# Expert weights split a whole raw tile at a time: one 2048-element split in place of two of 1024, with four pairs of buffers and six raw tiles

## The chip, the cores and the metric

The kernel runs on one core of one Trainium2 chip. The metric is device time in microseconds (us), the median of several runs. The core's engines are TensorE (PE, with its weight loads as PEld), VectorE (DVE), ScalarE (ACT), GpSimd (POOL) and SyncE (SP), which here issues the DMAs of the weights.

## What is computed

Two layers of a trunk over 272 tokens of width 1024: three token mixers in each layer, then a dense SwiGLU in the first layer and a mixture of eight experts, two per token, in the second. The change touches the experts alone:

```python
def swiglu(h, w_gate, w_up, w_down):
    return (jax.nn.silu(h @ w_gate) * (h @ w_up)) @ w_down

def moe_swiglu(h, router_w, w_gate, w_up, w_down):
    ...                       # top-2 of 8 experts, softmax weights in combine
    out = jnp.zeros_like(h)
    for e in range(N_EXPERTS):
        out = out + combine[..., e:e + 1] * swiglu(h, w_gate[e], w_up[e], w_down[e])
    return out
```

All weights are float32: 1024 x 3584 for gate and up, 3584 x 1024 for down, eight times; 352 MB in all.

## The kernel before

**Split products.** A float32 product is made from products of a shorter type (fp32r). Each operand is split into a high part (rounded) and a low part (the rest). For a piece of raw weights r, ACT writes the high part h (L855), DVE the low part l = r - h (L856), and PE multiplies with both. Every piece thus passes DMA, ACT, DVE and PE in this order.

**Experts.** The eight experts are ordered by their number of tokens. The four largest are "wide" (up to 128 tokens in one side; three products for each block of weights: h, l, and h once more with the tokens' low part, L1106 to L1108), the other four "narrow" (up to 64 tokens, whose high and low part lie side by side; two products: h, l, L1134 and L1135). The inner width 3584 is worked in 7 chunks of 512, so there are 28 wide and 28 narrow chunks. `order` (L1228 to L1231) begins with four wide chunks, then sets one narrow and one wide in turn (24 such pairs), and ends with the narrow ones that are left over.

**One chunk** (L1192 to L1219): two raw tiles of gate weights (g) are multiplied into `psg`, two of up weights (u) into `psu`, each of 1 MB and four blocks of 128 rows; then come two raw tiles of the down weights (d) of the chunk before it, two blocks each. Between them ACT reads the sums: in a narrow chunk `gs` from `psg` (L1140), `us` from `psu` (L1141) and, after PE has turned both (`hps`, L1149), the SiLU `s` (L78); in a wide chunk the SiLU `h` from `psg` (L78), which DVE multiplies by `psu` (L1113), and after PE's transposes `hth` (L1124). These readings stand in the same queues of ACT and DVE as the splits.

**Order.** The programmer writes the work in the order above. A planner of the framework lays out, when the program is built, the order of the instructions on each engine; it goes by its own idea of how long things take, and where the next product in the program's order isn't ready by its clock, it sets a later one that is. On the chip each engine then keeps to that order and waits at the head of its queue. Products into one PSUM tile keep the program's order.

**Buffers.** `RB` raw tiles of 8 KB per partition; `HB` pairs of h and l, of which the last `LATE` lie in a pool of their own. A raw tile is split in pieces of `st` blocks, 1024 elements per partition, so two pieces for each tile. A raw tile is free when both engines have read it, and a pair when PE has used it. The first `EARLY` pieces may be split before the router is done; those after them, up to the 15th, wait in the order for the router's instructions (L858 to L862).

Of the kernel before, what the change touches and what calls it, by code (L numbers as in the profile page):

```python
# [51 lines left out]
def trunk(ctx: ExitStack, tc: tile.TileContext, x, meta, n1g, n2g, w_in, qng, kng, dlam,  # L52
# [12 lines left out]
    def raw_ins(i):  # L65
        return getattr(i, "ins", i)
# [754 lines left out]
                    n1.add(dk, hs[:, dk, :])  # L821


    HB, RB, LATE, YB = 7, 7, 2, 1
    MT = dict(reuse_waits="tile")
    mo = ctx.enter_context(tc.tile_pool(name="mo", bufs=1, **MT))
    wqs = [ctx.enter_context(tc.tile_pool(name=f"wq{i}", bufs=1, **MT)) for i in range(2)]
# [6 lines left out]
        return pw.tile([P, 512], F32, tag="pw", name=name)  # L834

    nparts = [0]
    EARLY = 5

    class MoveWeights:

# [4 lines left out]
            nc.sync.dma_start(self.raw, src)  # L845

        def parts(self):
            st = 1024 // self.cols
            for k0 in range(0, self.nk, st):
                late = nparts[0] % HB >= HB - LATE  # L850
                wq, nb_ = (wqs[0], LATE) if late else (wqs[1], HB - LATE)
                hi = wq.tile([P, st, self.cols], F32R, tag="hi", bufs=nb_, name="h_" + self.name)
                lo = wq.tile([P, st, self.cols], F32R, tag="lo", bufs=nb_, name="l_" + self.name)
                r = self.raw[:, k0:k0 + st, :]
                ih = raw_ins(A.activation(hi, r, AF.Copy))  # L855
                il = raw_ins(V.tensor_tensor(lo, r, hi.bitcast(F32), op=ALU.subtract))  # L856
                nparts[0] += 1
                if EARLY < nparts[0] < 16:  # L858

                    tc.add_manual_dep(il, routed[0].name, nosync, reason="router")  # L860
                if EARLY < nparts[0] < 16:
                    tc.add_manual_dep(ih, last_in[0].name, nosync, reason="router")  # L862
                for k in range(st):
                    yield k0 + k, hi[:, k, :], lo[:, k, :]
# [404 lines left out]
```

## Time and profile before

| | us |
|---|---|
| median of 3 runs (1830.60 to 1834.19) | 1832.62 |
| the profiled execution, its own time | 1830.15 |
| its span | 1828.3 |
| of the span: before the first product of the experts' chunk 1, about | 860 |
| of the span: from the first narrow and wide pair to the last narrow chunk | 932.6 to 1793.3 |

The granted TensorE clock is 1.00 (2.4 GHz) in the experts' stretch. The view of windows gives each engine's busy time in a stretch; the view of waits says who waited for whom and how long; the timeline lists instructions in order of time, with the engine's idle time before one and what ended it in square brackets. PE's busy time counts matmuls to a modelled end, so two that follow each other overlap in it: their starts are 0.23 us apart while each is shown with about 0.4 us. One pair of chunks without other work in it, at 1677.3 to 1710.7 us, serves below as the pattern.

### The profile page before, as it was taken

What the parts mean: (1) busy time and instruction counts of PE and PEld (TensorE: products, weight loads), DVE (VectorE), ACT (ScalarE), POOL (GpSimd) and SP (SyncE); (2) the same over time, 40 slices, a digit from 0 to 9 for tenths busy, and PEclk for the clock granted to TensorE, in tenths of its full rate; (3) what the DMA queues carried; (4) which work ended last, traced back from release to release, by engine and by line L of the source; (5) the groups of instructions that cost most, each with busy time, mean ns of one, the idle gap of its engine ahead of it and who ended that gap; (6) DMA issues with size and microseconds to landing.
All of it is one profiled execution on the core that took longest, in us unless ns stands there. A gap on an engine that the chain in (4) does not pass through costs nothing.

```text
span 1828.3 us, 27950 instructions
## 1 busy us (share of the span) xinstructions
PE 1762.4 (96%) x10613; PEld 1508.4 (83%) x10613; DVE 1467.2 (80%) x1934; ACT 1173.2 (64%) x1587; POOL 110.6 (6%) x137
## 2 busy tenths in 40 slices
PE   8999999999999999999999999999999999999997
PEld 7888999999999889998888777766777767766765
DVE  7667757877567577578899998898998899889897
ACT  4366444544443664447788777777777777777786
POOL 5201201100011003012000000000000000000000
PEclk9999999999999999999999999999999999999999
DMA  7333554555554236657999999999999999999995
GB/s 215 102 97 93 170 176 162 165 181 185 167 178 140 70 95 189 186 197 257 335 366 388 349 372 375 338 364 381 360 366 342 367 377 362 370 366 344 373 375 205
DMA packets 266123, 479.96 MB, mean 263 GB/s; under 512 B 7636, under 2 KB 115228, under 8 KB 265980
## 3 DMA queue, kind: packets, MB, share of 16 engines
q1 hardware_dynamic: 265472, 477.20, 74.4%
q8 instruction: 85, 1.39, 0.3%
q0 software_dynamic: 368, 0.86, 0.2%
q14 instruction: 58, 0.48, 0.1%
q10 hardware_dynamic: 140, 0.04, 0.0%
HBM read 477.01 MB, written 1.05 MB: 261 GB/s over the span
## 4 chain that ended last, share of the span: by engine, by line
PE 45%; DVE 11%; ACT 7%; issue 3%; POOL 0%; ACTq 0%; DVEq 0%; POOLq 0%
DVE l_g L856 4%; ACT h_d L855 3%; DVE l_d L856 3%; PE psg L1107 3%; PE psg L1108 3%; PE psu L1135 3%; PE psg L1106 3%; PE psg L1135 3%; PE y L1106 2%; PE hps L1149 2%; PE psu L1134 2%; PE proj L230 2%; PE proj L229 2%; PE proj L228 2%; PE y L1107 2%
## 5 line engine op out<-in xcount | busy, mean ns | idle before, releaser
L230 PE MATMUL proj<-hgh,lo_in 128*128 128x272 f32 (+1 forms) x1024 | 296.9, 290 | 4.6 <-DVE lo_in L224 4.6
L228 PE MATMUL proj<-hgh,hi_in 128*128 128x272 f32 (+1 forms) x1024 | 297.5, 291 | 0.2 <-DVE z L357 0.2
L229 PE MATMUL proj<-hgl,hi_in 128*128 128x272 f32 (+1 forms) x1024 | 296.8, 290 | 0.0
L856 DVE TENSOR_TENSOR l_u<-r_u,h_u 128x1024 fp32r<-128x1024 f32 x224 | 265.4, 1221 | 34.4 <-ACT h_u L855 32.9
L856 DVE TENSOR_TENSOR l_d<-r_d,h_d 128x1024 fp32r<-128x1024 f32 x224 | 264.9, 1221 | 15.7 <-ACT h_d L855 14.5
L856 DVE TENSOR_TENSOR l_g<-r_g,h_g 128x1024 fp32r<-128x1024 f32 x224 | 264.9, 1223 | 10.2 <-ACT h_g L855 9.7
L223 ACT ACTIVATE hi_in<-raw_in 128x1024 fp32r<-128x1024 f32 x128 | 135.0, 1058 | 165.1 <-PE proj L229 149.8
L855 ACT ACTIVATE h_u<-r_u 128x1024 fp32r<-128x1024 f32 x224 | 225.2, 1050 | 5.4 <-PE y L1108 2.9
L855 ACT ACTIVATE h_g<-r_g 128x1024 fp32r<-128x1024 f32 x224 | 224.1, 1051 | 7.1 <-PE psu L1108 4.1
L855 ACT ACTIVATE h_d<-r_d 128x1024 fp32r<-128x1024 f32 x224 | 222.6, 1050 | 4.8 <-PE psg L1108 3.1
L230 PEld LDWEIGHTS proj<-hgh,lo_in 128*128 128x128 f32 x1024 | 193.7, 189 | 6.6 <-DVE lo_in L224 5.5
L228 PEld LDWEIGHTS proj<-hgh,hi_in 128*128 128x128 f32 x1024 | 193.8, 189 | 2.8 <-issue 1.1
L229 PEld LDWEIGHTS proj<-hgl,hi_in 128*128 128x128 f32 x1024 | 193.3, 189 | 2.4 <-issue 1.3
L224 DVE TENSOR_TENSOR lo_in<-raw_in,hi_in 128x1024 fp32r<-128x1024 f32 x128 | 158.7, 1242 | 33.3 <-ACT hi_in L223 33.0
L1135 PE MATMUL psg<-l_g,x 128*128 128x512 f32 x224 | 98.4, 439 | 17.5 <-DVE l_g L856 16.8
L1135 PE MATMUL psu<-l_u,x 128*128 128x512 f32 x224 | 97.1, 434 | 2.5 <-DVE l_u L856 2.4
L1107 PE MATMUL psg<-l_g,x 128*128 128x512 f32 x224 | 90.2, 403 | 1.5
L1107 PE MATMUL y<-l_d,hth 128*128 128x512 f32 x224 | 89.3, 398 | 1.6 <-DVE l_d L856 1.6
L1134 PE MATMUL psu<-h_u,x 128*128 128x512 f32 x224 | 90.3, 403 | 0.0
L1107 PE MATMUL psu<-l_u,x 128*128 128x512 f32 x224 | 90.1, 402 | 0.1
L1135 PEld LDWEIGHTS psg<-l_g,x 128*128 128x128 f32 x224 | 41.9, 187 | 57.7 <-DVE l_g L856 51.6
L1134 PE MATMUL psg<-h_g,x 128*128 128x512 f32 x224 | 88.9, 397 | 0.0
(404 smaller groups left out, 4105.9 us busy)
## 6 DMA issues: line engine op xcount, KB each, us to landing
r_g<-in_moe_w_gate_dram SPq DMA_DIRECT2D x112, 1024.0 KB, 7.7
r_u<-in_moe_w_up_dram SPq DMA_DIRECT2D x112, 1024.0 KB, 7.0
r_d<-in_moe_w_down_dram SPq DMA_DIRECT2D x110, 1024.0 KB, 6.6
raw_in<-in_w_in_dram SPq DMA_DIRECT2D x64, 1024.0 KB, 6.0
raw_br<-in_w_branch_dram SPq DMA_DIRECT2D x12, 1024.0 KB, 5.3
raw_fg<-in_ffn_w_gate_dram SPq DMA_DIRECT2D x11, 1024.0 KB, 5.4
raw_fu<-in_ffn_w_up_dram SPq DMA_DIRECT2D x11, 1024.0 KB
raw_wo<-in_w_out_dram SPq DMA_DIRECT2D x8, 1024.0 KB, 4.9
```

What stands on the lines that cost most here:

```text
L223: A.activation(hi, r, AF.Copy)
L224: V.tensor_tensor(lo, r, hi.bitcast(F32), op=ALU.subtract)
L228: PE.matmul(ps, sh, mh, start=first, stop=False)
L229: PE.matmul(ps, sh, ml, start=False, stop=False)
L230: PE.matmul(ps, sl, mh, start=False, stop=last)
L855: ih = raw_ins(A.activation(hi, r, AF.Copy))
L856: il = raw_ins(V.tensor_tensor(lo, r, hi.bitcast(F32), op=ALU.subtract))
L1106: PE.matmul(ps, st[0], hi, start=first, stop=False)
L1107: PE.matmul(ps, st[0], lo, start=False, stop=False)
L1108: PE.matmul(ps, st[1], hi, start=False, stop=last)
L1134: PE.matmul(ps, st[0], hi, start=first, stop=False)
L1135: PE.matmul(ps, st[0], lo, start=False, stop=last)
```

## The change

One piece is now a whole raw tile: `st` is 2048 over the number of columns, and no more than the tile has (the last four d tiles have one block and stay at 1024 elements). There are four pairs in place of seven, each twice as large, one of them in the pool of its own in place of two; and six raw tiles in place of seven. 112 KB per partition stay 112 KB. The bounds for the router's order go from 5 and 16 pieces of half a tile to 3 and 9 of a whole one. The splits fall from 672 to 338 on ACT and DVE each.

```diff
-    HB, RB, LATE, YB = 7, 7, 2, 1
+    HB, RB, LATE, YB = 4, 6, 1, 1
...
-    EARLY = 5
+    EARLY = 3
...
         def parts(self):
-            st = 1024 // self.cols
+            st = min(2048 // self.cols, self.nk)
             for k0 in range(0, self.nk, st):
                 late = nparts[0] % HB >= HB - LATE
                 wq, nb_ = (wqs[0], LATE) if late else (wqs[1], HB - LATE)
...
-                if EARLY < nparts[0] < 16:
+                if EARLY < nparts[0] < 9:
                     tc.add_manual_dep(il, routed[0].name, nosync, reason="router")
-                if EARLY < nparts[0] < 16:
+                if EARLY < nparts[0] < 9:
                     tc.add_manual_dep(ih, last_in[0].name, nosync, reason="router")
```

## Rows read from the trace of the kernel before

**Rows 1.** The page, part 1: busy time, share of the span, instructions of each engine.
```profile
PE 1762.4 (96%) x10613; PEld 1508.4 (83%) x10613; DVE 1467.2 (80%) x1934; ACT 1173.2 (64%) x1587; POOL 110.6 (6%) x137
```

**Rows 2.** Windows: stretch, length; busy PE, PEld, DVE, ACT, POOL; PE clock; DMA share, GB/s.
```profile
932.60:1793.30 860.70, 830.31 (x3715) 630.36 (x3714) 776.18 (x783) 669.28 (x801) 0.00 (x0) 1.00 1.00 365
1677.30:1710.70 33.40, 32.41 (x142) 23.93 (x141) 29.65 (x29) 25.99 (x31) 0.00 (x0) 1.00 1.01 371
```

**Rows 3.** Waits, 900 to 1800 us: who for whom, us in total, times, longest.
```profile
PEld psg L1135 <- DVE l_g L856: 51.6, 92, 1.5
ACT gs L1140 <- PE psg L1135: 42.3, 22, 3.4
...
ACT h L78 <- PE psg L1108: 33.6, 21, 3.7
DVE l_u L856 <- ACT h_u L855: 30.7, 44, 1.3
```

**Rows 4.** Timeline of ACT in the pattern pair: start, length, instruction, count, [idle before].
```profile
1677.31 3.89 ACT L855 ACTIVATE h_g<-r_g 128x1024 fp32r<-128x1024 f32 x4
...
1685.31 0.69 ACT L1140 ACTIVATE gs<-psg,ws 128x512 f32<-128x512 f32 x1 [2.21 <-PE psg L1135]
1685.89 2.00 ACT L855 ACTIVATE h_u<-r_u 128x1024 fp32r<-128x1024 f32 x2
...
1690.38 0.60 ACT L1141 ACTIVATE us<-psu 128x512 f32<-128x512 f32 x1 [0.60 <-PE psu L1135]
...
1702.64 0.69 ACT L78 ACTIVATE h<-psg,ws 128x512 f32<-128x512 f32 x1 [1.85 <-PE psg L1108]
...
1710.72 1.05 ACT L855 ACTIVATE h_g<-r_g 128x1024 fp32r<-128x1024 f32 x1
```

**Rows 5.** Timeline of DVE in the pattern pair.
```profile
1679.63 4.62 DVE L856 TENSOR_TENSOR l_g<-r_g,h_g 128x1024 fp32r<-128x1024 f32 x4
1684.17 2.35 DVE L856 TENSOR_TENSOR l_u<-r_u,h_u 128x1024 fp32r<-128x1024 f32 x2
1686.97 2.36 DVE L856 TENSOR_TENSOR l_u<-r_u,h_u 128x1024 fp32r<-128x1024 f32 x2 [0.45 <-ACT h_u L855]
...
1691.96 2.36 DVE L856 TENSOR_TENSOR l_d<-r_d,h_d 128x1024 fp32r<-128x1024 f32 x2 [0.36 <-ACT h_d L855]
...
1704.31 2.36 DVE L856 TENSOR_TENSOR l_u<-r_u,h_u 128x1024 fp32r<-128x1024 f32 x2 [1.29 <-ACT h_u L855]
```

**Rows 6.** Timeline of PE in the pattern pair's narrow chunk.
```profile
1684.31 0.50 PE L1135 MATMUL psg<-l_g,x 128*128 128x512 f32 x1
...
1684.87 0.39 PE L1135 MATMUL psg<-l_g,x 128*128 128x512 f32 x1
...
1687.41 0.40 PE L1135 MATMUL psu<-l_u,x 128*128 128x512 f32 x1
1687.65 0.33 PE L1149 MATMUL hps<-ii,gs 128*128 128x64 f32 x2
1687.79 0.48 PE L1134 MATMUL psu<-h_u,x 128*128 128x512 f32 x1
1688.11 0.33 PE L1149 MATMUL hps<-ii,gs 128*128 128x64 f32 x2
```

**Rows 7.** Groups by shape: count, busy us, mean ns of one, idle before.
```profile
L856 DVE TENSOR_TENSOR l_u<-r_u,h_u 128x1024 fp32r<-128x1024 f32 x209 | 247.2, 1221 | 31.8 <-ACT h_u L855 30.7
L855 ACT ACTIVATE h_u<-r_u 128x1024 fp32r<-128x1024 f32 x210 | 210.5, 1050 | 3.5 <-PE y L1108 2.0 <-PE psg L1108 1.2 <-ACT h_u L855 0.3
...
L78 ACT ACTIVATE gt<-gt 128x2048 f32<-128x2048 f32 x3 | 5.7, 1904 | 0.0
...
L224 DVE TENSOR_TENSOR lo_fd<-raw_fd,hi_fd 128x768 fp32r<-128x768 f32 x8 | 7.7, 959 | 14.4 <-ACT hi_fd L223 14.4
```

**Rows 8.** The weights' DMAs (L845), 900 to 1800 us: SP's largest wait; landing.
```profile
SPq L845 <- DVE l_u L856: 227.3, 100, 5.4
...
DMA to landing us min/median/max: 5.0/7.5/10.6
```

## The prediction

> **What bounds the kernel now.** I read part 1 of the page, then the windows of the experts' stretch, the waits there, and the timelines of one clean pair of chunks. Part 1 alone would name PE: 96% [rows 1]. That figure misleads here: products start 0.23 us apart but are shown with 0.39 to 0.50 us each [rows 6], so a PE that is late now and then still looks full. In the pattern pair, 33.40 us, PE issues 48 narrow and 72 wide products, 120 x 0.23 = 27.6 us, and some 2 us of turning (8 records each for `gs` and `us`, two of which hold the next product up by 0.14 us [rows 6], and 4 transposes): about 30 us of 33.4. DVE is busy 29.65 us [rows 2]. The DMA engines show a share of 1.00, but they don't set the pace: SP waits to issue (227.3 us for one tile kind's release alone), so raw buffers are full, not empty [rows 8], and ACT's splits hardly ever wait: 3.5 us before 210 of them [rows 7].
>
> No engine is saturated, then; what costs the last 3 us of a pair is a ring of waits. PE waits for DVE's low parts, DVE for ACT's high parts, and ACT, with a reading of PSUM at the head of its queue, for PE [rows 3]. The first such ring in the pair: the last low part of g ends at 1684.25 (1679.63 + 4.62) [rows 5]; PE starts three products at 1684.31, the last at 1684.87 and done at 1685.26 [rows 6]; `gs` starts at 1685.31, the next split behind it at 1685.89 [rows 4], and DVE gets work at 1686.97, 2.72 us after it finished g. The one tile between had kept it busy until 1686.52: a stall of 0.45 [rows 5]. The same ring at `us` costs 0.36 and at the wide `h` 1.29 [rows 5].
>
> **The price of one split.** On ACT two of 1024 take 2.00 us [rows 4] and one of 2048 takes 1.90 [rows 7]. On DVE two take 2.35 [rows 5]; one of 2048 isn't in the trace. From 768 to 1024 elements it grows by 0.262 us for 256 [rows 7], so 1024 more cost 1.05 and one of 2048 takes 2.27. That saves 0.08 us a tile, 1.0 us a pair of twelve tiles on DVE, some 24 us over 24 pairs if DVE were never late. Bounds: nothing (if the growth were 1.13 per 1024), and 1.7 us a pair (if each of two were paid alone, 2 x 1.221 - 2.27 = 0.17, minus what they overlap).
>
> The Trainium skill, "Perfetto Trace Analysis", section "Optimizing Scalar/DVE Operations", has a rule for either outcome: grouping into larger operations helps where the engine is saturated, with some 60 ns for each instruction on DVE, and breaking instructions up helps where ACT and DVE aren't saturated but cause bubbles on other engines. By the first rule the sum would be about 334 x 0.06 = 20 us less, as an estimate from that page; by the second it would be a loss. The rows of waits speak for the second.
>
> **What the larger piece adds to a ring.** It is waited for as a whole. After the last low part of a narrow gate tile PE now has seven products left, not three (l h l h l h l): 4 x 0.23 = 0.92 us more. The split behind the reading is done after 1.90, not 1.05: 0.85 more. DVE gets work 2.72 + 0.92 + 0.85 = 4.49 us after it finished g, and one tile covers 2.19 of that. The stall goes from 0.45 to 2.30: +1.85. At `us` likewise, +1.85.
>
> **Whether one tile or two lie in between.** This decides, and it is the planner's. In the pair each reading stands at the edge of a tile, behind the first tile that follows its sum; so the planner seems to pace ACT by the arrival of raw tiles. How far apart it takes them to be can be read from PE's order: after the last product of the first u tile (1687.41) it set two turning products, then the first of the next tile, then two more [rows 6]. Turning comes later in the program, so by the planner's clock the second tile's first high part was done 0 to 0.3 us after the first tile's last product. With this trace's durations, counted from a tile's arrival: second low part 1.05 + 1.14 + 1.22 = 3.4, three products 0.7, sum 4.1; the next tile's first high part comes at T + 1.05. T is then 3.05 to 3.35 us (real pace 33.4 / 12 = 2.8). After the change a narrow gate sum is done, from the arrival of its last tile, at 1.90 + 2.27, a step of 0.06 and seven products, 0.56 + 4 x 0.23 + 0.39 = 1.87, together 6.1; the second tile after it arrives at 2T = 6.1 to 6.7. So `gs` stays behind one tile, by a narrow margin, and `us` by the same sum. A wide sum needs four more products: 7.0, past 2T; `h` should move behind two tiles. There DVE has two low parts, 4.4 us, to cover what the ring asks, so of the 1.29 stall I take 1.1 away (bounds: 0, and all 1.29).
>
> **The sum for a pair:** +1.85 at `gs`, +1.85 at `us`, -1.0 for fewer instructions, -1.1 at `h`: +1.6 us. The narrow part is where it is lost; in the wide part PE, at 12 x 0.23 = 2.76 us a tile against DVE's 2.27, sets the pace before and after. 24 pairs: +38. The narrow chunks left over at the end have no wide part to recover in: three full ones at 2 x 1.85 - 0.5 = +3.2: +10. The total is +48: the profiled execution would go from 1830.15 to 1878 (its span is 1.9 below its time), and the median, 2.5 above it, from 1832.62 to 1880.
>
> **The other edits.** Six raw tiles in place of seven: a tile's DMA is issued when the tile that held its buffer is through DVE. With six, its own split begins about 6 x 2.9 - 4.2 = 13 us later; landing takes 7.5, at most 10.6 [rows 8]. So it is hidden, with 2.6 us over the slowest; no other work queues behind these issues on SP in the steady part. If that cover went, each late tile would hold ACT by its excess. Nothing at all, up to 2 us for a tile in a hundred. Pairs: four whole ones let ACT lead PE by four tiles, seven halves by three and a half; ACT waits for a free one for 3.5 us in 210 splits [rows 7], so I take nothing; below by as much, above by one split, 0.85, in each of the first four wide chunks. The router's bounds: three tiles before it, not two and a half; the splits that may delay its chain are 0.85 (ACT) and 1.05 (DVE) longer, once or twice: -2 to +3, taken as 0. The last four d tiles don't change.
>
> **Rivals.** First, faster: all readings move back a tile, which happens if the planner's T is under 3.05. Then two low parts, 4.4 us, face a ring of 4.49: stalls of 0.1 in place of 0.45 and 0.36. The gain is at least the shorter splits, 1.0 a pair, 24 us: 1808; at most also the stalls (0.35 + 0.26 + 1.1), 65 us. I take the small end, since `s` and `hth` come later too. For it: the margin above is as small as its uncertainty, and the real pace, 2.8, lies below it. Against: the order of PE's products. The Trainium skill's rule on larger operations (same page and section) would then hold.
>
> Second, much slower: `h` stays behind one tile as well (T over 3.5). Then it too pays 1.85 and gives nothing back: 3 x 1.85 - 1.0 = +4.55 a pair, +109 +10: 1952. For it: T may be larger than its bound if the planner's splits are slower than the chip's. Against: 7.0 against 6.7 at most.
>
> Third, no change: PE, 30 us of 33.4, has slack that takes up the longer rings, and the 24 us of shorter splits pay for the rest: 1833. Against it: DVE's stalls in the narrow part are on the path now, since each is followed by PE's wait for the low part [rows 3].
>
> **How the numbers follow.** Forecast 0.60, own range 1848 to 1915 (+0.6 to +3.0 a pair: the bounds of the splits' price, of the stall at `h`, and of `us` alone moving back, which spares one 1.85 but costs at the next reading). Much slower 0.20 (1930 to 1965). Faster 0.15. No change 0.05. The range of 1842 to 1955 leaves out the faster case and a little at the top. A measurement of this kernel tells about 0.2% from no change: faster 0.15, same 0.05, slower 0.80.
>
> **What would show it.** Right: one-piece splits of 1.90 and about 2.27 us; in the timeline of ACT `gs` behind one u tile and DVE idle there by some 2.3 us, at `us` by 2.2; a pair near 35.0 us; DVE busy about 1 us less a pair; ACT's splits still not waiting for landings. Wrong: `gs` behind both u tiles and DVE idle for a few tenths only (first rival); `h` behind one tile (second); or ACT waiting for raw tiles, which would make six too few.

## The result: 3.1% slower

The changed kernel takes 1887.8 us (median; 1884.90 to 1890.51) beside 1831.6 us for the kernel before in the same runs: a ratio of 1.031, with a 95% interval of 1.028 to 1.033. The forecast was 1880. The profiled execution has a span of 1888.0 us against 1828.3, so there are 59.7 us to find. Both traces cut at the same products, the first gate product of the first narrow chunk and that of the first narrow chunk left over:

| stretch | before, us | after, us | difference | forecast |
|---|---|---|---|---|
| up to the first narrow and wide pair | 925.1 | 929.9 | +4.8 | 0 |
| the 24 pairs | 821.4 | 865.9 | +44.4 | +38 |
| the narrow chunks left over, to the end | 81.8 | 92.3 | +10.5 | +10 |

A cut at ACT's first split of each narrow chunk, as the times 860, 932.6, 1677.3 and 1710.7 above have it, would give +40.8 for the pairs and +14.1 for the tail, since at the start of the tail that split stands 2.1 us ahead of PE's first product before and 5.8 us after. (So too the 860 above is ACT's first split for chunk 1, whose first product comes at 868.9.) Pairs are therefore cut at products here and below.

Cut once more at the first gate product of the wide chunk, the narrow halves of the 24 pairs go from 413.3 to 474.4 us and the wide halves from 408.2 to 391.5, so all of the loss is in the narrow halves, as forecast. The 44.4 are spread unevenly. Four pairs grew by 5.0, 5.1, 4.3 and 3.9 us, 18.3 together; the other twenty by 26.1 in all, each between -3.2 and +6.1.

Part 1 of the page after, and the windows of all pairs, of the pattern pair (the same two chunks as in [rows 2]) and of one of the four costly ones; columns as in [rows 2]:

```profile
PE 1764.2 (93%) x10613; PEld 1523.0 (81%) x10613; DVE 1438.7 (76%) x1600; ACT 1140.0 (60%) x1253; POOL 114.3 (6%) x137
...
929.90:1795.75 865.85, 789.88 (x3552) 613.02 (x3551) 716.64 (x461) 611.21 (x476) 0.00 (x0) 0.99 0.96 347
1725.60:1760.70 35.10, 31.77 (x142) 24.20 (x140) 28.68 (x17) 25.18 (x19) 0.00 (x0) 1.00 0.98 355
1283.90:1324.00 40.10, 33.65 (x142) 25.16 (x141) 31.55 (x22) 24.75 (x19) 0.00 (x0) 0.96 0.89 312
```

ACT and DVE do less (DVE 28.5 us less than in [rows 1]) and the kernel is slower. In the pattern pair DVE is busy 28.68 us where it was busy 29.65 (33.40 us long and 29.65 busy in either cut), and idle for 6.42 where it had been idle for 3.75: 1.0 us of work saved, 2.7 us of waiting added, and the pair is 1.7 us longer.

The new pieces cost what was worked out. Groups by shape (count, busy us, mean ns of one):

```profile
L856 DVE TENSOR_TENSOR l_u<-r_u,h_u 128x2048 fp32r<-128x2048 f32 x112 | 254.6, 2287 | 52.5 <-ACT h_u L855 52.4
...
L855 ACT ACTIVATE h_u<-r_u 128x2048 fp32r<-128x2048 f32 x112 | 211.2, 1907 | 12.9 <-PE y L1108 6.5 <-DMA r_u<-in_moe_w_up_dram 2.8 <-PE y L1134 2.0
```

The second line also shows ACT waiting for a landing for 2.8 us in all: six raw tiles are nearly enough. Where the waiting went is in the waits of 900 to 1850 us (who for whom, us in total, times, longest), to be held against [rows 3]:

```profile
DVE l_d L856 <- ACT h_d L855: 80.0, 47, 3.5
ACT us L1141 <- PE psu L1135: 55.2, 22, 3.8
ACT gs L1140 <- PE psg L1135: 54.0, 22, 4.0
...
DVE l_u L856 <- ACT h_u L855: 48.9, 27, 3.2
PEld psg L1135 <- DVE l_g L856: 46.5, 44, 2.0
PEld psu L1135 <- DVE l_u L856: 37.5, 28, 2.1
ACT h L78 <- PE psg L1108: 35.4, 22, 2.0
```

It is the same ring of PE, ACT and DVE as before, with larger waits for fewer pieces. In the timelines of the pattern pair after, ACT first and then DVE (start, length, instruction, count, idle before), the three rings are seen one by one, as in [rows 4, 5]:

```profile
1731.04 0.69 ACT L1140 ACTIVATE gs<-psg,ws 128x512 f32<-128x512 f32 x1 [2.70 <-PE psg L1135]
1731.62 1.90 ACT L855 ACTIVATE h_u<-r_u 128x2048 fp32r<-128x2048 f32 x1
...
1737.84 0.60 ACT L1141 ACTIVATE us<-psu 128x512 f32<-128x512 f32 x1 [2.51 <-PE psu L1135]
...
1745.07 3.70 ACT L855 ACTIVATE h_u<-r_u 128x2048 fp32r<-128x2048 f32 x2
1750.73 0.69 ACT L78 ACTIVATE h<-psg,ws 128x512 f32<-128x512 f32 x1 [1.97 <-PE psg L1108]
```

```profile
1733.56 2.29 DVE L856 TENSOR_TENSOR l_u<-r_u,h_u 128x2048 fp32r<-128x2048 f32 x1 [2.30 <-ACT h_u L855]
...
1740.27 2.29 DVE L856 TENSOR_TENSOR l_d<-r_d,h_d 128x2048 fp32r<-128x2048 f32 x1 [2.22 <-ACT h_d L855]
...
1745.35 2.29 DVE L856 TENSOR_TENSOR l_g<-r_g,h_g 128x2048 fp32r<-128x2048 f32 x1
1747.55 4.49 DVE L856 TENSOR_TENSOR l_u<-r_u,h_u 128x2048 fp32r<-128x2048 f32 x2
1753.26 2.29 DVE L856 TENSOR_TENSOR l_d<-r_d,h_d 128x2048 fp32r<-128x2048 f32 x1 [1.22 <-ACT h_d L855]
```

`gs` and `us` each stand one tile behind their sum, and DVE idles there for 2.30 and 2.22 us. `h` has moved behind both u tiles, and DVE still idles 1.22 us for it. Around `s` the waiting has gone, and at DVE's product of `h` and `psu` it has stayed, as two more stretches of DVE's timeline show, before and then after:

```profile
1694.83 0.42 DVE L1152 TENSOR_TENSOR s<-s,hps 128x256 f32<-128x256 f32 x1 [0.51 <-ACT s L78]
1695.78 2.36 DVE L856 TENSOR_TENSOR l_g<-r_g,h_g 128x1024 fp32r<-128x1024 f32 x2 [0.53 <-ACT h_g L855]
...
1708.42 0.69 DVE L1113 TENSOR_TENSOR h<-h,psu 128x512 f32<-128x512 f32 x1 [0.61 <-PE psu L1108]
```

```profile
1742.48 0.41 DVE L1152 TENSOR_TENSOR s<-s,hps 128x256 f32<-128x256 f32 x1
1742.81 2.29 DVE L856 TENSOR_TENSOR l_g<-r_g,h_g 128x2048 fp32r<-128x2048 f32 x1
...
1756.23 0.69 DVE L1113 TENSOR_TENSOR h<-h,psu 128x512 f32<-128x512 f32 x1 [0.68 <-PE psu L1108]
```

### The profile page after: what moved, and what is told of

Its sections match the earlier page's. It is cut to its first block, busy times and chain, and to the rows that moved or that the text cites. A ratio compares the mean times of both kernels' runs of the same rounds, so it can differ in the third digit from the quotient of the medians.

```text
span 1888.0 us, 27076 instructions
## 1 busy us (share of the span) xinstructions
PE 1764.2 (93%) x10613; PEld 1523.0 (81%) x10613; DVE 1438.7 (76%) x1600; ACT 1140.0 (60%) x1253; POOL 114.3 (6%) x137
## 4 chain that ended last, share of the span: by engine, by line
PE 39%; DVE 14%; ACT 8%; issue 5%; POOL 0%; ACTq 0%; DVEq 0%; POOLq 0%
DVE l_d L856 4%; ACT h_d L855 4%; DVE l_g L856 4%; DVE l_u L856 3%; PE psg L1107 3%; PE psg L1108 2%; PE psg L1106 2%; PE psu L1135 2%; ACT h_g L855 2%; PE y L1107 2%; ACT h_u L855 2%; PE proj L229 2%; PE proj L230 2%; PE proj L228 2%; PE y L1108 2%
## 5 line engine op out<-in xcount | busy, mean ns | idle before, releaser
L856 DVE TENSOR_TENSOR l_d<-r_d,h_d 128x2048 fp32r<-128x2048 f32 (+1 forms) x114 | 256.1, 2250 | 84.8 <-ACT h_d L855 84.8
L856 DVE TENSOR_TENSOR l_u<-r_u,h_u 128x2048 fp32r<-128x2048 f32 x112 | 254.6, 2287 | 52.5 <-ACT h_u L855 52.4
L856 DVE TENSOR_TENSOR l_g<-r_g,h_g 128x2048 fp32r<-128x2048 f32 x112 | 255.5, 2286 | 19.0 <-ACT h_g L855 19.0
L855 ACT ACTIVATE h_g<-r_g 128x2048 fp32r<-128x2048 f32 x112 | 213.5, 1910 | 11.6 <-PE psu L1108 6.9
L855 ACT ACTIVATE h_u<-r_u 128x2048 fp32r<-128x2048 f32 x112 | 211.2, 1907 | 12.9 <-PE y L1108 6.5
L855 ACT ACTIVATE h_d<-r_d 128x2048 fp32r<-128x2048 f32 (+1 forms) x114 | 212.3, 1877 | 4.8 <-PE psg L1108 2.5
L1135 PE MATMUL psg<-l_g,x 128*128 128x512 f32 x224 | 93.8, 419 | 31.0 <-DVE l_g L856 30.8
L1107 PE MATMUL psg<-l_g,x 128*128 128x512 f32 x224 | 89.7, 400 | 0.6 <-DVE l_g L856 0.6
L1135 PE MATMUL y<-l_d,ht 128*128 128x512 f32 x224 | 83.7, 405 | 5.9 <-DVE l_d L856 5.7
```

The lines of the kernel that those rows point to most:

```text
L1107: PE.matmul(ps, st[0], lo, start=False, stop=False)
L1135: PE.matmul(ps, st[0], lo, start=False, stop=last)
```

## The experiments

All of them do the whole of the work; only pieces, buffers and order differ. Times are medians; a ratio is to the kernel before on the same chip (1830 to 1831 us). "Pair" is the mean of the two clean pairs at the end (33.4 before, 35.1 after). Three theories stood against each other. Theory 1: a piece that is twice as large lengthens the ring of waits. Theory 2: four pairs and six raw tiles are fewer stations than seven and seven, and engines wait for buffers. Theory 3: the larger piece matters only because the planner puts ACT's readings of PSUM one tile behind their sums.

### Size or buffers

`e1` keeps everything of the change (four whole pairs, six raw tiles, the router's bounds) but splits a tile with two instructions of 1024 on each engine (`halves` are the tile's first and second half):

```diff
-                ih = raw_ins(A.activation(hi, r, AF.Copy))
-                il = raw_ins(V.tensor_tensor(lo, r, hi.bitcast(F32), op=ALU.subtract))
+                ihs = [raw_ins(A.activation(hi[:, q, :], r[:, q, :], AF.Copy)) for q in halves]
+                ils = [raw_ins(V.tensor_tensor(lo[:, q, :], r[:, q, :], hi[:, q, :].bitcast(F32), op=ALU.subtract)) for q in halves]
```

> The changed kernel with its buffers kept (four whole pairs, six raw tiles, the same bounds for the router), but each tile split by two instructions of half a tile on ACT and two on DVE, so that a product waits for half a tile again. Theory 1, the size of the piece (what is waited for, and the order that follows from it): the clean pair goes back from 34.6 to 33.4 us, DVE's stalls at gs and us to 0.45 and 0.36, and the time to 1832 (1824 to 1842). Theory 2, the buffers (six raw tiles land too late, or four pairs hold ACT back): nothing is given back, 1875 to 1895, and ACT's or SP's waits show it.

Measured: 1830.9, ratio 1.0004 (0.9994 to 1.0014), pair 33.4, and the engines' order is that of the kernel before but for some places ahead of the pairs and in the first three. The waits are back as well:

```profile
PEld psg L1137 <- DVE l_g L856: 51.7, 92, 1.5
ACT gs L1142 <- PE psg L1137: 40.0, 22, 3.4
...
DVE l_u L856 <- ACT h_u L855: 32.5, 47, 1.3
```

Theory 2 falls: the buffers cost nothing, and all of the 3.1% is the size of the pieces, with the order that the planner makes of it. That holds for the start too: ACT's first split for chunk 1 stands at 860.0 before, 864.9 after and 859.7 here.

### Which engine's piece

`e2` splits with one instruction on ACT and two on DVE, `e3` the other way round.

> The changed kernel with ACT's split of a whole tile and DVE's in two halves. It takes one of the two added terms away, PE's wait for the whole low part (0.92 us a ring), and keeps the other, the whole high part behind a reading (0.85 us). Theory 1: the stall at gs is 0.45 + 0.85 = 1.3 us, not 2.3; the pair lies between before and after unless the planner moves a reading, some 1855 to 1880. If PE's wait alone were the cause: 1832. If the high part alone: 1888.

> The changed kernel with DVE's split of a whole tile and ACT's in two halves. DVE still waits for both halves of the high part, 2.0 us, so theory 1 expects nothing back: the stall at gs stays at 2.3 us or a little over, 1880 to 1895. If ACT's long instruction were what holds the readings up, 1850 to 1870.

Measured: `e2` 1897.1, ratio 1.036 (1.034 to 1.038), pair 36.4; `e3` 1869.8, ratio 1.021 (1.020 to 1.023), pair 34.5. Both missed, and both for the same reason: the planner laid out another order. In `e2` it set `h` back behind one u tile and `s` behind one d tile, and ACT and DVE pay for the first in the wide part:

```profile
ACT h L78 <- PE psg L1110: 83.8, 25, 5.3
DVE l_u L856 <- ACT h_u L855: 71.9, 43, 3.1
```

In `e3` it set `us` half a tile later than in the changed kernel and `s` a gate tile later; `h` kept its place. So these two don't price a piece; each prices a piece together with an order.

`e5` is `e2` with `h` and `s` held to their places in after (`h` behind both u tiles, `s` behind both d tiles), by dependences that order two instructions and add no wait. `gs` and `us` stand as in after; `hth` still comes one gate tile earlier.

> ACT's split of a whole tile, DVE's in two halves, as in the run with the low part in halves, but with the readings h and s held at the places that they have in the changed kernel (h behind both u tiles, s behind both d tiles), so that the size of the low part alone differs from it. Theory 1: PE's wait for a whole low part (0.92 us a ring) is gone and the whole high part behind the reading (0.85) stays; the stalls at gs and us come to 1.3 and 1.2 us in place of 2.30 and 2.22, and after 1.0 us a pair for twice the instructions on DVE the pair is about 33.6 and the time 1850 to 1870. If the low part's size were no matter once the order is the same: 1885 to 1895.

Measured: 1860.1, ratio 1.016 (1.014 to 1.017), pair 34.1. With these readings held, DVE's halves take about half of the loss away; what the place of `hth` has in that was not tried. The other half stays with ACT's whole piece and the order that goes with it. `e2` against `e5` shows what two readings' places alone are worth: 37 us.

### The readings' places

`e4` is after, with `gs` and `h` set behind both u tiles and `us` behind both d tiles, again by such dependences alone. `h` stands there in after already, so what moves is `gs` and `us`, and the planner set `s` a gate tile later with them:

```diff
     # in parts(): last_split[:] = [ih]
+    def behind(i):
+        tc.add_manual_dep(i, last_split[0].name, nosync, reason="late")
...
-            act(h, psg, AF.Silu, scale=self.g.ws[:, 0, 1:2])
+            behind(act(h, psg, AF.Silu, scale=self.g.ws[:, 0, 1:2]))
...
-            A.activation(gs, psg, AF.Copy, scale=self.g.ws[:, 1, 1:2])
-            A.activation(us, psu, AF.Copy)
+            behind(raw_ins(A.activation(gs, psg, AF.Copy, scale=self.g.ws[:, 1, 1:2])))
+            self.late = lambda: behind(raw_ins(A.activation(us, psu, AF.Copy)))   # called after the d tiles
```

`e6` does the same to the kernel before, where `h` moves too, and `e7` to whole pieces on ACT with halves on DVE.

> The changed kernel with the readings set later on ACT: gs and h behind both u tiles, us behind both d tiles (an order alone, no wait on another engine; all the work is done). Two low parts, 4.4 us, then cover a ring of 4.5. Theory 1: the stalls at gs and us fall from 2.3 to some 0.1 to 0.3 us and the time goes below the kernel before, to 1805 to 1835, which is the faster rival of the prediction brought about by hand. If the whole-tile pieces cost time by themselves, whatever stands between them (PE's wait for a whole low part in every tile): 1860 to 1890.

> The kernel before, halves, seven pairs, seven raw tiles, with the readings set later on ACT as in the run with whole tiles: gs and h behind both u tiles, us behind both d tiles. A ring of 2.7 us is then covered by 4.5 us of low parts. Theory 1: the stalls at gs, us and h (0.45 + 0.36 + 1.29) go; the pair falls from 33.4 to 31.3 to 32.0 us and the time to 1785 to 1812, below the whole-tile kernel with later readings (1823.7), since its rings are shorter. If the later order pays only together with whole tiles and their fewer instructions: 1820 to 1832.

> The changed kernel with later readings and DVE's split in two halves. Where two low parts cover a ring anyway the size of the low part should matter less: theory 1 expects 1810 to 1830, within 1% of the run with whole low parts (1823.7); a loss as large as without later readings (9 us more than the changed kernel) would give 1833.

Measured: `e4` 1823.7, ratio 0.996 (0.995 to 0.998), pair 32.2; `e7` 1825.7, ratio 0.997 (0.996 to 0.998), pair 32.6; both within what was expected. `e6` 1829.3, ratio 0.999 (0.998 to 1.000), pair 33.1, far from the 1785 to 1812 expected and within the 1820 to 1832 of the other reading. Theory 3 holds for the whole pieces: 64 us between after and `e4` come from the places of `gs` and `us` and of what moved with them. `e6` shows the stalls at `gs`, `us` and `h` gone, and two others in their place, both in this timeline of DVE:

```profile
1692.04 0.42 DVE L1158 TENSOR_TENSOR s<-s,hps 128x256 f32<-128x256 f32 x1 [1.91 <-ACT s L78]
...
1702.62 0.69 DVE L1119 TENSOR_TENSOR h<-h,psu 128x512 f32<-128x512 f32 x1 [1.26 <-PE psu L1114]
```

ACT's reading `s` waits for the turning, which now comes later (83.4 us of such waits, 39.6 before), and DVE's product of `h` and `psu` waits for PE.

### The next stalls

`e8` (halves) and `e9` (whole) add `s` behind both next g tiles; `e10` and `e11` further put DVE's product of `h` and `psu` behind both d tiles' low parts. The halves of `e6`, `e8` and `e10` have the buffers of the kernel before:

```diff
-            act(s, hps[:, 0:256], AF.Silu)
+            behind(act(s, hps[:, 0:256], AF.Silu))            # e8 to e11
...
-            V.tensor_tensor(h, h, psu, op=ALU.mult)
+            self.late = lambda: behind(raw_ins(V.tensor_tensor(h, h, psu, op=ALU.mult)), 1)   # e10, e11
```

> Halves with later readings, and s now behind both gate tiles of the next chunk as well. In the run with halves and later readings the stalls at gs, us and h were gone, but ACT stood 4.5 us at s behind one gate tile, DVE 1.9 us behind it. If that ring took the place of the others: the pair falls from 33.2 to 31.0 to 32.3 us and the time from 1829 to 1790 to 1815. If PE's own work holds the pair by now: within 3 us of 1829.

> Whole tiles with later readings, and s behind both gate tiles of the next chunk. There DVE still stood 0.35 and 1.17 us a pair before low parts of g, behind ACT's wait at s. The ring theory: the pair from 31.9 to 30.6 to 31.5 us, the time from 1823.7 to 1795 to 1818. If PE's own work, some 30 us a pair, holds it: 1820 to 1826.

> Halves as in the run with s later too, and DVE's product of h and psu behind the low parts of both d tiles. It takes away DVE's wait of 1.26 us for psu in the wide part. If DVE's stalls there count: 10 to 25 us below the run without it; if PE sets the pace in the wide part, as the prediction took it: within 6 us of that run.

> Whole tiles as in the run with s later too, and DVE's product of h and psu behind the low parts of both d tiles. DVE's wait for psu, 0.68 us a pair, goes. If PE sets the pace in the wide part: within 6 us of the run without it; later transposes may cost as much.

Measured: `e8` 1825.9, ratio 0.997 (0.996 to 0.998), pair 32.9; `e9` 1822.6, ratio 0.995 (0.993 to 0.997), pair 32.2. Moving `s` is worth some 3 us at most, far less than the ring theory expected of it. In `e8` the stall went straight on to the product (39.3 us of waits, up from 19.5 in `e6`), as DVE's timeline shows:

```profile
1701.66 0.69 DVE L1119 TENSOR_TENSOR h<-h,psu 128x512 f32<-128x512 f32 x1 [2.60 <-PE psu L1114]
```

With this wait moved too, `e10` takes 1807.6, ratio 0.987 (0.985 to 0.988), pair 31.9, and `e11` 1798.3, ratio 0.982 (0.980 to 0.984), pair 31.5: 18 and 24 us for the place of one DVE instruction in the wide part and of what follows from it (PE's transposes of the product and `hth` come later too). `e11` is the fastest kernel of this study. In a pair of its chunks DVE is left with two stalls, of 0.54 and 2.37 us:

```profile
1661.01 4.49 DVE L860 TENSOR_TENSOR l_d<-r_d,h_d 128x2048 fp32r<-128x2048 f32 x2
1666.03 4.49 DVE L860 TENSOR_TENSOR l_g<-r_g,h_g 128x2048 fp32r<-128x2048 f32 x2 [0.54 <-ACT h_g L859]
...
1673.31 2.28 DVE L860 TENSOR_TENSOR l_u<-r_u,h_u 128x2048 fp32r<-128x2048 f32 x1
1677.96 4.50 DVE L860 TENSOR_TENSOR l_d<-r_d,h_d 128x2048 fp32r<-128x2048 f32 x2 [2.37 <-ACT h_d L859]
1682.37 0.68 DVE L1119 TENSOR_TENSOR h<-h,psu 128x512 f32<-128x512 f32 x1
```

Halves (the kernel before, `e6`, `e8`, `e10`) and whole tiles (after, `e4`, `e9`, `e11`), with the same readings held later; the rest of the order, as the place of `hth`, is the planner's and differs between the columns:

| order | halves, us | whole, us |
|---|---|---|
| the planner's own | 1831 | 1888 |
| `gs`, `us`, `h` later | 1829 | 1824 |
| `s` later too | 1826 | 1823 |
| DVE's product later too | 1808 | 1798 |

The whole tile loses 3.1% in the first row. In the second it wins by a ratio of 0.9963 (up to 0.9977) against 0.9988 (from 0.9979), in the last by 0.982 (up to 0.984) against 0.987 (from 0.985); in the third the intervals overlap.

## Why the prediction was right, and where only its sum was

**The price of a split** was right: 1.907 us on ACT (1.90 forecast) and 2.287 on DVE (2.27). The pattern pair's DVE is busy 1.0 us less, as worked out.

**The ring at `gs` and `us`** was right to a few hundredths: 2.30 and 2.22 us idle, where 2.30 and 2.2 were forecast (0.45 + 1.85, 0.36 + 1.85). Counting the products that PE has left after the last low part, and the whole split that ACT still has to do behind its reading, is what gives this. `e4` showed that these two stalls are on the path (the one at `h` is 1.10 us there, much as after), and `e1` that the piece alone makes them.

**The planner's order** was read rightly from PE's order in the trace of before: `gs` and `us` one tile behind, `h` behind both. The first rival (every reading a tile later) didn't come about by itself; `e4` made it on purpose, and it took 1824, not 1808. Its step failed where it let the stalls vanish: `s`, `ht` and the product of `h` became late instead. The second rival's mechanism is what `e2` ran into, at 1897.

**The term for `h`** was mis-sized: 1.1 us were to go, and 0.07 went (1.29 to 1.22). I set the narrow part's ring of 4.49 us against two low parts. The wide ring is longer, since PE has eleven products left there, not seven: DVE ends the last g tile at 1747.64 (1745.35 + 2.29) and gets new work at 1753.26, 5.62 us later, of which the two u tiles cover 4.40. What made up for it were two stalls that I hadn't listed, 0.51 us at `s` and 0.53 at the split behind it: they went away (over 900 to 1850 us DVE's waits for `s` fell from 16.1 to 3.4 us). So `gs`, `us` and `h` add 3.6 us of idle time, `s` takes 1.0 back, the shorter splits another 1.0, and the clean pair came out at +1.7 for +1.6. That this is so close is luck: two errors of 1.0 us cancelled.

**"In the wide part PE sets the pace"** was wrong. `e8` to `e10` and `e9` to `e11` gained 18 and 24 us by moving one DVE instruction that waits there for PE with splits queued behind it. The wide half of a clean pair holds 64 products, 14.7 us at 0.23, and four transposes; it takes 16.6 us before, 15.7 after and 14.6 in `e11`, where the transposes stand in the narrow half: only there does PE set its pace. A PE share of 93% or 96% doesn't say that PE is never kept waiting.

**The costly pairs** were not foreseen at all. In each of them PE fell to its lower clock (below). Three of the four hold the combine of a wide expert's output, where ACT reads PSUM once more (`yh`); in the fourth gathered tokens' sums (`gat`) are read. DVE's timeline of one of them, after, and of the same pair in `e4`:

```profile
1293.09 2.29 DVE L856 TENSOR_TENSOR l_u<-r_u,h_u 128x2048 fp32r<-128x2048 f32 x1 [2.30 <-ACT h_u L855]
...
1301.11 2.29 DVE L856 TENSOR_TENSOR l_d<-r_d,h_d 128x2048 fp32r<-128x2048 f32 x1 [3.52 <-ACT h_d L855]
...
1306.10 0.75 DVE L1079 SCALAR_TENSOR_TENSOR yl<-y,ws,yh 128x512 fp32r<-128x512 f32 x1 [0.49 <-ACT yh L1078]
1307.90 2.29 DVE L856 TENSOR_TENSOR l_g<-r_g,h_g 128x2048 fp32r<-128x2048 f32 x1 [1.05 <-ACT h_g L855]
```

```profile
1280.15 0.75 DVE L1085 SCALAR_TENSOR_TENSOR yl<-y,ws,yh 128x512 fp32r<-128x512 f32 x1 [1.02 <-ACT yh L1084]
1281.96 2.29 DVE L860 TENSOR_TENSOR l_g<-r_g,h_g 128x2048 fp32r<-128x2048 f32 x1 [1.05 <-ACT h_g L859]
```

The stall at `gs` is that of a clean pair, the one at `us` is 1.3 us longer, its products having run at the lower clock, and `yh` adds a ring of 1.5 us that the kernel before doesn't have there. But `yh` is not what makes the pair costly. `e4` leaves it where it is, its ring costs 2.1 us there, and the three pairs take 35.0, 35.0 and 34.4 us beside 35.1, 35.1 and 34.5 before (40.1, 40.2 and 38.4 after); and the three pairs that begin with the same reading for a narrow expert are 0.4 to 0.6 us shorter after than before. So what `e4` changed, the places of `gs` and `us`, takes the excess away, and with it three of the four stretches at the lower clock. The pair with `gat` takes 34.2 us before, 38.5 after and 36.1 in `e4`; the fourth such stretch, worth 1.7 us, is still there.

My sum was for a pair without such work, times 24. The four costly pairs added 18.3 us where it has 6.4, the other twenty 26.1 where it has 32. That the total, 44.4, is near 38 is therefore partly luck.

**The tail** came to +10.5 for +10, though not as 3.2 us for each of three chunks: the four chunks left over grew by 4.1, 0.9, 3.6 and 1.8, and the first of them holds one more stretch at the lower clock. `e4` has 80.9 us there (92.3 after, 81.8 before).

**The other edits.** Six raw tiles cost 2.8 us of waits in two places, at most; pairs nothing (`e1`). The router's part was bounded by -2 to +3 and taken as 0; it cost 4.8. `e1` shows that this comes from the size of the pieces and not from the bounds, since it has the same bounds; which of the router's instructions the longer splits delay was not followed.

The Trainium skill, "Perfetto Trace Analysis", section "Optimizing Scalar/DVE Operations", has both rules at once: grouping into larger operations helps a saturated engine, and breaking them up helps where ACT and DVE aren't saturated but cause bubbles elsewhere. For the change as it was made the traces agree with the second: DVE at 80%, and 56 us lost by grouping. Once the readings stand later, grouping gains: whole tiles win by 9 us in the last row, with DVE at 80% in `e11`, not saturated, a case that neither rule names.

## What to carry to other kernels

Before making a piece larger, write down the ring that it passes through: the engine that makes it, the products behind it, the reading of their sum, and the next piece behind that reading; the larger piece adds its growth to each engine in the ring, and what decides is whether one tile or two lie between a sum and its reading. When an experiment changes a piece in a kernel whose order a planner lays out, hold the order, or it prices two things at once. Stalls in a ring pass on to the next wait, so judge by the time and not by the one stall that has gone: here later readings brought 64 us with whole tiles and almost nothing with halves, until DVE's product was moved too.

## What the runs showed of the chip

A PE that waits can get a lower clock, and then a stall costs more than its length. In the costly pair the windows show the granted clock (the column behind POOL's) fall to 0.64 on average at 1294 to 1298.8 us, and in the pattern pair's like stretch it stays:

```profile
1294.00:1298.80 4.80, 3.36 (x9) 2.69 (x10) 3.59 (x2) 0.98 (x2) 0.00 (x0) 0.64 0.99 347
...
1728.40:1736.00 7.60, 5.25 (x26) 3.83 (x25) 5.30 (x4) 4.29 (x3) 0.00 (x0) 1.00 1.02 372
```

Microsecond by microsecond it is 0.50 there, 1.2 GHz, and PE's timeline has products 0.43 us apart in place of 0.23:

```profile
1293.11 0.50 PE L1134 MATMUL psu<-h_u,x 128*128 128x512 f32 x1 [0.38 <-ACT h_u L855]
1295.44 0.79 PE L1135 MATMUL psu<-l_u,x 128*128 128x512 f32 x1 [1.82 <-DVE l_u L856]
1296.03 0.63 PE L1134 MATMUL psu<-h_u,x 128*128 128x512 f32 x1
1296.46 0.63 PE L1135 MATMUL psu<-l_u,x 128*128 128x512 f32 x1
```

The clock fell at 1294.9, in the second of two waits of PE, 0.38 and 1.82 us, with one product in between. The same two waits, within 0.02 us, come just before two of the other falls in the pairs; before the one in the pair with `gat` PE waited 1.40 us. In the pattern pair, where the waits at the same place are 0.54 and 1.13 us and eight turning products and eight others lie in between, it doesn't fall. After has four such stretches within the pairs, each 3.4 us long and each in one of the four costly pairs; the kernel before has none there, `e1` and `e11` neither, and `e4` one. Nor has `e2`, the slowest kernel of all, so the lower clock is not what makes a kernel slow here. Summed over the four, (1 - clock) x time is 6.8 us, over a third of the 18.3 by which these pairs grew.
